# A decoder trunk whose attention layer keeps its tokens by residue class, with the attention values made as seven block products

## The chip, the cores and the metric

One core of a Trainium2 chip runs the whole program. The metric is device time in microseconds of one execution. Five engines matter: TensorE (PE) with its weight loads (PEld), VectorE (DVE), ScalarE (ACT), GpSimd (POOL), and SyncE (SP), which here only issues transfers.

## The reference, cut to what matters

512 tokens of width 1024 pass through two layers. Layer 0 mixes tokens by attention, layer 1 by causal pooling; each is followed by a SwiGLU feed-forward of width 2816.

```python
ATTN_PAIRS = ((128, 1), (512, 4), (2048, 16))     # (window, dilation), 3 groups of 8 heads
def dilated_window_attention(q, k, v, window, dil, slopes):
    # query t attends to keys t - j*dil, j = 0..window/dil; ALiBi bias, softmax
    ...
    o = jnp.einsum('bnhqk,bnkhd->bnqhd', p / den, vb)
    lse = (m + jnp.log(den))[..., 0].transpose(0, 1, 3, 2)
    ...
def dilated_attention_mixer(h, w_qkv, w_out):
    qkv = (h @ w_qkv).reshape(B, S, 3, 3, 8, 128)           # group, q/k/v, head
    ...
    wts = jax.nn.softmax(jnp.stack(lses, axis=0), axis=0)   # over the three groups
    o = jnp.sum(wts[..., None] * o, axis=0).reshape(B, S, ATTN_WIDTH)
    return o.astype(h.dtype) @ w_out
def reference(x, ...):
    x = x + dilated_attention_mixer(rmsnorm(x, attn_norm), w_qkv, w_attn_out)
    x = x + swiglu_ffn(rmsnorm(x, ffn_norm[0]), ...)
    x = x + pooling_mixer(rmsnorm(x, pool_norm), ...)
    x = x + swiglu_ffn(rmsnorm(x, ffn_norm[1]), ...)
    return rmsnorm(x, final_norm)
```

A group with dilation 4 splits the 512 tokens into four residue classes of 128, and the group with dilation 16 works inside the same classes with a stricter mask. Both are called the folded groups below; the group with dilation 1 is the first group.

## The kernel before, in words

**Numbers.** Activations lie transposed: 128 channels on the partitions, 512 tokens along the free dimension, eight such tiles for 1024 channels. Each f32 operand is split into a rounded part (hi, made by ACT, L78) and the rest (lo, made by DVE, L79), and a product is three fp32r products: hi by hi, hi by lo, lo by hi (L245 to L248). Scores, the products with the values and the turning of tiles use full f32; each full-f32 product is two instructions in the trace.

**Weights.** A list of units is built before the program starts. A `Plain` unit is one load of up to 1024 columns and one split. A `Pair` unit (L122) serves a Strassen-Winograd form of two products at once, over 2 x 2 blocks of 512 channels by 256 tokens: three loads from SP and one adding load from POOL, then four steps (blocks, sums, more, last) that make the weight tiles b, s, m and l. Rings of five full and two half split tiles, and four full and two half raw tiles, set how far ahead this runs; `pump` (L165) moves the list on between products.

**Block products.** `seven` (L393) makes two products of 512 columns as seven half products of 4 x 3 matmuls of 256 columns, and DVE adds them up. In the attention layer it serves q and k of heads 1 to 7 (head 1 after its plain start); the feed-forwards use it too. A view (`Straight`, `Folded`) tells it to write a folded group's result with the tokens reordered by residue class.

**Attention.** Head by head q and k of three groups are made; after heads 0, 2, 4, 6 `values` (L496) makes the first group's values of two heads, after heads 1, 3, 5, 7 `values12` (L473) makes those of both folded groups for two heads. In both the normed activations are the stationary operand and the weights the moving one: `values` takes 4 blocks of tokens x 8 chunks x 3 matmuls of 256 columns, `values12` 8 chunks x 4 classes x 3 matmuls of 512 columns, and picks a class out of H with a stride of four tokens. Around these, `between` (L737) and the lists handed to the stages place the other steps of a head: `scores0` (L530) and `scores12` (L564) for scores, exponentials and statistics, which go through DRAM to change between token order and class order; `merge` (L591) for the weights of the groups; `turn` (L611) for transposed probabilities; `output` (L629) for the products with the values, where the folded part is added with a reordering view on DVE (L650). The engines' orders are settled when the program is built, from this order and what is ready.

**Start.** Four leading products run as chunks of x arrive (L709 to L724). Ten instructions on an idle tile (five products, L708) come before. Then a whole product (L725), the sums of squares over channels (`rstd`, L303, one product with a column of ones per 128 tokens), three steps of another product, and the row of scales (`spread`).

**Later stages.** The rest is the output projection, feed-forward 0, the pooling layer and feed-forward 1. The adds into x at the end of a feed-forward are L903.

## Time and profile before

| what | us |
|---|---|
| median of three runs | 1284.84 (1280.31 to 1288.69) |
| the profiled execution | 1277.5 |
| its span, first to last instruction | 1275.7 |
| PE busy in the span | 1262.7 |
| DVE busy | 866.3 |
| ACT busy | 529.4 |
| attention's period for two heads, 206 to 317 | 111.0 |

The granted clock of the profiled execution is 0.998. In a row of time order the first number is the start and the second the length of a group of like instructions, in us; `a<-b,c` names what is written and read, for a matmul the moving and then the stationary operand. In a row of groups the two numbers before the last bar are the busy time in us and the mean length of one in ns. Lengths of matmuls overlap, so a matmul's price is the distance to the next start. A row of stages gives the stretch, its length, then busy time and number of instructions for each engine, the granted clock, the share of the transfer engines, and GB/s. A row of waits gives the total, the number and the longest.

### The profile page before, as it was taken

What the parts mean: (1) busy time and instruction counts of PE and PEld (TensorE: products, weight loads), DVE (VectorE), ACT (ScalarE), POOL (GpSimd) and SP (SyncE); (2) the same over time, 40 slices, a digit from 0 to 9 for tenths busy, and PEclk for the clock granted to TensorE, in tenths of its full rate; (3) what the DMA queues carried; (4) which work ended last, traced back from release to release, by engine and by line L of the source; (5) the groups of instructions that cost most, each with busy time, mean ns of one, the idle gap of its engine ahead of it and who ended that gap; (6) DMA issues with size and microseconds to landing.
All of it is one profiled execution on the core that took longest, in us unless ns stands there. A gap on an engine that the chain in (4) does not pass through costs nothing.

```text
span 1275.7 us, 20125 instructions
## 1 busy us (share of the span) xinstructions
PE 1262.7 (99%) x8036; PEld 1165.3 (91%) x8036; DVE 866.3 (68%) x1313; ACT 529.4 (41%) x825; POOL 106.4 (8%) x105
## 2 busy tenths in 40 slices
PE   9999999999999999999999999999999999999997
PEld 7989999999999998889989999888788988999986
DVE  6794876658566637578636887458978853788643
ACT  6443444444344424445324454333443532455331
POOL 1101101010110100001001110000300000111000
PEclk9999999999999999999999999999999999999999
DMA  8143546446644713147346774333124645676222
GB/s 292 52 142 75 149 133 137 124 110 159 119 117 134 179 53 124 58 100 183 121 141 156 187 180 126 108 139 116 50 67 111 173 139 132 173 182 170 95 69 66
DMA packets 83454, 163.88 MB, mean 128 GB/s; under 512 B 27440, under 2 KB 29504, under 8 KB 83360
## 3 DMA queue, kind: packets, MB, share of 16 engines
q1 hardware_dynamic: 67792, 132.82, 33.4%
q0 software_dynamic: 14416, 28.72, 13.5%
q8 instruction: 63, 1.03, 0.3%
q10 hardware_dynamic: 1152, 1.05, 0.2%
q14 instruction: 31, 0.25, 0.1%
HBM read 160.40 MB, written 2.16 MB: 127 GB/s over the span
## 4 chain that ended last, share of the span: by engine, by line
PE 80%; issue 10%; DVE 6%; DMA 2%; ACT 1%; POOL 1%; SPq 0%; DVEq 0%; POOLq 0%; ACTq 0%
PE ps L385 12%; PE ps L384 12%; PE ps L386 12%; PE ps L245 9%; PE ps L248 9%; PE ps L246 9%; PE ps L484 2%; PE ps L485 2%; PE ps L486 2%; DVE wlo L79 2%; PE ps L647 1%; PE ps L510 1%; PE ps L509 1%; PE ps L511 1%; PE ps L573 1%
## 5 line engine op out<-in xcount | busy, mean ns | idle before, releaser
L79 DVE TENSOR_TENSOR wlo<-raw,whi 128x1024 fp32r<-128x1024 f32 (+2 forms) x286 | 327.0, 1146 | 199.9 <-ACT whi L78 198.8
L78 ACT ACTIVATE whi<-raw 128x1024 fp32r<-128x1024 f32 (+2 forms) x286 | 283.9, 998 | 420.8 <-PE ps L246 203.0
L245 PE MATMUL ps<-a,whi 128*128 128x512 f32 (+1 forms) x374 | 141.0, 377 | 0.0
L246 PE MATMUL ps<-a,whi 128*128 128x512 f32 (+1 forms) x374 | 140.9, 377 | 0.0
L248 PE MATMUL ps<-a,wlo 128*128 128x512 f32 (+1 forms) x374 | 140.8, 377 | 0.0
L384 PE MATMUL ps<-tt,whi 128*128 128x256 f32 x384 | 108.7, 283 | 0.0
L385 PE MATMUL ps<-tt,whi 128*128 128x256 f32 x384 | 108.7, 283 | 0.0
L386 PE MATMUL ps<-tt,wlo 128*128 128x256 f32 x384 | 108.7, 283 | 0.0
L248 PEld LDWEIGHTS ps<-a,wlo 128*128 128x128 f32 x374 | 70.4, 188 | 12.9
L246 PEld LDWEIGHTS ps<-a,whi 128*128 128x128 f32 x374 | 70.4, 188 | 12.8
L245 PEld LDWEIGHTS ps<-a,whi 128*128 128x128 f32 x374 | 70.4, 188 | 12.7
L137 POOL DMA_DIRECT2D raw<-w_pair x32 | 38.3, 1197 | 445.7 <-DVE wlo L79 168.2
L384 PEld LDWEIGHTS ps<-tt,whi 128*128 128x128 f32 x384 | 73.7, 192 | 0.0
L385 PEld LDWEIGHTS ps<-tt,whi 128*128 128x128 f32 x384 | 73.7, 192 | 0.0
L386 PEld LDWEIGHTS ps<-tt,wlo 128*128 128x128 f32 x384 | 73.7, 192 | 0.0
L385 PE MATMUL ps<-tb,whi 128*128 128x256 f32 x256 | 72.6, 284 | 0.5 <-DVE tb L79 0.5
L386 PE MATMUL ps<-tb,wlo 128*128 128x256 f32 x256 | 72.4, 283 | 0.0
L384 PE MATMUL ps<-tb,whi 128*128 128x256 f32 x256 | 72.4, 283 | 0.0
L245 PE MATMUL ps<-h,whi 128*128 128x512 f32 x160 | 62.7, 392 | 0.0
L248 PE MATMUL ps<-h,wlo 128*128 128x512 f32 x160 | 62.3, 389 | 0.0
L246 PE MATMUL ps<-h,whi 128*128 128x512 f32 x160 | 62.3, 389 | 0.0
L384 PE MATMUL ps<-h,whi 128*128 128x256 f32 x216 | 61.9, 286 | 0.0
(247 smaller groups left out, 3329.7 us busy)
## 6 DMA issues: line engine op xcount, KB each, us to landing
raw<-w_pair SPq DMA_DIRECT2D x76, 512.0 KB, 4.2
raw<-w_qkp SPq DMA_DIRECT2D x36, 512.0 KB, 4.7
raw<-w_pair POOLq DMA_DIRECT2D x32, 512.0 KB, 7.1
raw<-w_v SPq DMA_DIRECT2D x24, 512.0 KB, 3.5
raw<-w_down SPq DMA_DIRECT2D x32, 384.0 KB, 3.1
raw<-w_down SPq DMA_DIRECT2D x32, 320.0 KB, 2.8
raw<-w_qkp POOLq DMA_DIRECT2D x18, 512.0 KB, 7.3
rawhalf<-w_pair SPq DMA_DIRECT2D x32, 256.0 KB, 3.3
```

The source lines that it names most:

```text
L78: nc.scalar.activation(hi, v, AF.Copy)
L79: nc.vector.tensor_tensor(lo, v, hi.bitcast(F32), op=OP.subtract)
L137: nc.gpsimd.dma_start(self.b.t.rearrange("p (a c) -> p a c", a=2), self.src[:, None, 3 * S:].to_broadcast([P, 2, S]), accum_op=OP.add)
L245: nc.tensor.matmul(self.p[:, cols], w[0][:, s], mh[:, cols], start=self.done == 0, stop=False)
L246: nc.tensor.matmul(self.p[:, cols], w[0][:, s], ml[:, cols], start=False, stop=False)
L248: nc.tensor.matmul(self.p[:, cols], w[1][:, s], mh[:, cols], start=False, stop=self.done == self.n)
L384: nc.tensor.matmul(dst, w.t[0][:, c], th, start=k == 0, stop=False)
L385: nc.tensor.matmul(dst, w.t[0][:, c], tl, start=False, stop=False)
L386: nc.tensor.matmul(dst, w.t[1][:, c], th, start=False, stop=k == K2 - 1)
L484: nc.tensor.matmul(ps4[b], oph[:, b, :], wh, start=k == 0, stop=False)
L485: nc.tensor.matmul(ps4[b], oph[:, b, :], wl, start=False, stop=False)
L486: nc.tensor.matmul(ps4[b], opl[:, b, :], wh, start=False, stop=k == KC - 1)
```

## The change

**Token order.** In layer 0 tokens lie by residue class: position r * 128 + i * 4 + b holds token b * 128 + i * 4 + r. So x, H, the tiles of sums and everything made from them have each class adjacent, and `block` picks one of the first group's blocks of 128 tokens with a stride of four. The host reorders x and the distance tables to match. The reordering views of `seven`, of head 0's evacuations and of `output` go; `block` comes into head 0's `values`, the first group's scores (both operands), the sums of squares, the row of scales and one ACT copy of `output`. The small transfers of statistics change their patterns. At the end of feed-forward 0 `unfold` adds into x with tokens back in their natural order, into tiles shifted by one, and ACT copies one of them.

**Values.** `values12` becomes the seven block products over two pairs of weights, with activations stationary: 7 x 2 x 4 x 3 matmuls of 256 columns, ACT making one copy and DVE seven sums and differences. The first group's values of heads 2, 4 and 6 become one `seven` with the weights stationary, so they come out transposed, and `turn_values` turns them by eight transposes after the next head's first block product. Head 0's stay plain.

**Order.** Scores of the folded groups and merges are attached to other points of the stages. The start loads the identity and distances from SP after the first weights instead of from POOL before them, runs six idle products instead of five, and makes the sixth product (`begin(1, 0, range(KC))`) after head 0's first evacuations instead of before the sums of squares.

On PE at the start, in the program's names (`early` are the scaled activations, `acc` the sums of squares, `ident` the identity), before:

```order
L245 MATMUL ps_300<-early_94,whi_309 128x512
L246 MATMUL ps_300<-early_95,whi_309 128x512
L248 MATMUL ps_300<-early_94,wlo_310 128x512
L309 MATMUL ps_349<-ones_79,acc_298 128x1 x4
L245 MATMUL ps_358<-early_88,whi_339 128x512 [waits Activation_49]
...
L322 MATMUL ps_383<-ident_78,rcol_356 128x128 [waits DMASW2_49,PE_49,Pool_49]
```

and now:

```order
L257 MATMUL ps_102<-early_95,whi_252 128x512
L259 MATMUL ps_102<-early_94,wlo_253 128x512
L323 MATMUL ps_301<-ones_79,acc_296 128x1 [waits DVE_49]
L323 MATMUL ps_301<-ones_79,acc_296 128x1 x3
L256 MATMUL ps_310<-early_88,whi_319 128x512 [waits Activation_49]
...
L336 MATMUL ps_347<-ident_78,rcol_308 128x128 [waits DMAHW1_49,Pool_49]
```

The sums of squares follow directly on the four leading products, and the row of scales now waits for a transfer from SP's queue.

On DVE in the folded values of heads 2 and 3, where the statistics of a head are merged (`mx`, `ex`), weights are split (`wlo`) and scores prepared (`s`), before:

```order
L575 SCALAR_TENSOR_TENSOR s_2177<-ps,b_2004 128x512 [waits PE_49]
L580 TENSOR_REDUCE st<-s_2177 128x4 [waits DVE_49]
L581 TENSOR_SCALAR nm<-st 128x4 [waits DVE_49]
L79 TENSOR_TENSOR wlo<-raw,whi 128x1024 [waits Activation_49]
L598 TENSOR_TENSOR mx<-st 128x8 [waits DMAHW7_49,DMAHW3_49]
L599 TENSOR_TENSOR ex<-st,mx 128x16 [waits DVE_49]
```

and now (`v` are the values, `sums` and `first` scratch):

```order
L617 TENSOR_SCALAR nm<-st 128x4 [waits DVE_49]
L493 TENSOR_TENSOR v_2268<-ps,first 128x2x256 [waits PE_49,Activation_49]
L80 TENSOR_TENSOR wlo<-raw,whi 128x1024 [waits Activation_49]
L80 TENSOR_TENSOR wlo<-raw,whi 128x1024 [waits DMAHW6_49,Activation_49]
L152 TENSOR_TENSOR raw<-raw 128x512 [waits DMAHW3_49,DMASW3_49,DVE_49]
L153 TENSOR_TENSOR raw<-raw 128x512 [waits DVE_49]
L80 TENSOR_TENSOR wlo<-raw,whi 128x1024 [waits Activation_49] x2
L634 TENSOR_TENSOR mx<-st 128x8 [waits DMAHW7_49,DMAHW4_49]
L635 TENSOR_TENSOR ex<-st,mx 128x16 [waits DVE_49]
L503 TENSOR_TENSOR sums<-ps,first 128x512 [waits PE_49]
```

The merge stands behind three more splits, two sums and an evacuation, and the stage's own evacuations stand behind it.

The diff, cut to its core:

```diff
-WARM = 5
+WARM = 6
...
-            steps.extend([(self, "w", self.blocks), (self, "w", self.sums), (self, "w", self.more),
-                          (self, "half", self.last)])
+        def steps(self):
+            return [(self, "w", self.blocks), (self, "w", self.sums), (self, "w", self.more), (self, "half", self.last)]
...
+    def pairs(*srcs):
+        these = [Pair(src) for src in srcs]
+        for parts in zip(*(p.steps() for p in these)):
+            steps.extend(parts)
+        units.append(these)
...
-        if h % 2 == 0:
-            plain(*[w_v0[h // 2, i] for i in range(2)])
+        if h == 0:
+            plain(w_v0[0], w_v0[1])
+        elif h % 2 == 0:
+            pairs(w_v0p[h // 2 - 1])
         else:
-            plain(*[w_v12[h // 2, i] for i in range(4)])
+            pairs(w_v12[h // 2, 0], w_v12[h // 2, 1])
...
-                nc.tensor.matmul(pc[:, t:t + 1], a[:, t * P:(t + 1) * P], ones,
+                nc.tensor.matmul(pc[:, t:t + 1], block(a, t), ones,
...
-    fold = "p (i r) -> p r i"
-    unfold = "p (r i) -> p r i"
+    def block(t, b, n=1):
+        v = t.rearrange("p (i b) -> p b i", b=NT)
+        return v[:, b] if n == 1 else v[:, b:b + n]
...
+                def product(name, half, key):
+                    p = ps()
+                    for a in range(2):
+                        for k in range(K2):
+                            wh, wl = (v[:, half * S + k % 2 * H2:half * S + (k % 2 + 1) * H2]
+                                      for v in part(unit[k // 2], name).t)
+                            mh, ml = (blk(v, a) for v in T[key, k])
+                            o = both(p)[:, a]
+                            nc.tensor.matmul(o, mh, wh, start=k == 0, stop=False)
+                            nc.tensor.matmul(o, mh, wl, start=False, stop=False)
+                            nc.tensor.matmul(o, ml, wh, start=False, stop=k == K2 - 1)
+                        pump()
+                    return p
...
+                m1 = product("b", 0, "11")
+                first = scratch("first")
+                nc.scalar.copy(first, m1)
+                behind(0)
+                m2 = product("b", 1, "21")
+                nc.vector.tensor_add(quarter(0, 0), both(m2), both(first))
+                done("b")
+                behind(1)
+                m5 = product("s", 0, "1")
...
+                m7 = product("s", 1, "3")
...
+                m6 = product("m", 0, "2")
+                u2 = scratch("sums")
+                nc.vector.tensor_add(u2, m6, first)
+                u3 = scratch("sums")
+                nc.vector.tensor_add(u3, m7, u2)
+                nc.vector.tensor_sub(quarter(1, 1), both(m5), both(u3))
...
-                        mh, ml = (blk(v, b) for v in of(k))
+                        mh, ml = (block(v, b) for v in of(k))
...
+            def turn_values(h):
+                t = apool.tile([P, NT, 2 * P], F32, name="v0")
+                for c in range(2):
+                    p = ps()
+                    for b in range(NT):
+                        nc.tensor.transpose(blk(p, b), block(VT[c], b), ident)
+                    nc.scalar.copy(t[:, :, c * P:(c + 1) * P], p.rearrange("p (b d) -> p b d", b=NT))
+                QKV[h // 2, 0, 2] = t
...
-                    nc.tensor.matmul(blk(p, 2 * b - 2, 2), blk(q0, b), blk(k0, b - 1, 2), start=True, stop=True)
+                    nc.tensor.matmul(blk(p, 2 * b - 2, 2), block(q0, b), block(k0, b - 1, 2), start=True, stop=True)
...
-                nc.tensor.matmul(blk(p, 0, 2), blk(q0, 3), blk(k0, 2, 2), start=True, stop=True)
-                nc.tensor.matmul(blk(p, 2), blk(q0, 0), blk(k0, 0), start=True, stop=True)
+                nc.tensor.matmul(blk(p, 0, 2), block(q0, 3), block(k0, 2, 2), start=True, stop=True)
+                nc.tensor.matmul(blk(p, 2), block(q0, 0), block(k0, 0), start=True, stop=True)
...
-                    nc.sync.dma_start(dn.rearrange("s (b p) -> p s b", p=P), st[:, 0, 0])
-                    nc.sync.dma_start(st[:, 1, 1], dn.rearrange("s (i r) -> i s r", r=4))
+                    nc.sync.dma_start(dn.rearrange("s (p b) -> p s b", b=NT), st[:, 0, 0])
+                    nc.sync.dma_start(st[:, 1, 1], dn.rearrange("s (r p) -> p s r", r=NT))
...
-                nc.scalar.copy(o0, po)
+                nc.scalar.copy(block(o0, 0, NT), po.rearrange("p (b i) -> p b i", b=NT))
...
-                nc.vector.tensor_add(o0.rearrange(fold, r=4), o0.rearrange(fold, r=4), po.rearrange(unfold, r=4))
+                nc.vector.tensor_add(o0, o0, po)
...
-            lead += begin(1, 0, range(KC))
-            rcol = rstd([acc[0]])
+            nc.sync.dma_start(ident, ident_in)
+            nc.sync.dma_start(d0, dist0)
+            nc.sync.dma_start(d12, dist12)
+            rcol = rstd([acc[0]], block)
...
-                    return {0: [later(merge, h - 1)], 1: [later(turn, h - 1), later(scores0, h)], 2: []}[g]
+                    return {0: [later(merge, h - 1), later(turn_values, h - 1)],
+                            1: [later(turn, h - 1), later(scores0, h)], 2: []}[g]
...
                 if h % 2 == 0:
-                    QKV[h // 2, 0, 2] = values(lambda k: H[k], None, {0: [later(scores12, h)]})
+                    VT[:] = [apool.tile([P, S], F32, tag=tag, name="vt") for tag in ("row", "o0")]
+                    seven(T, *VT, scratch, {0: [later(scores12, h)]})
                 elif h < HEADS - 1:
-                    QKV[h // 2, 12, 2] = values12({1: [later(scores12, h)], 5 if h > 1 else 7: [later(merge, h)]})
+                    QKV[h // 2, 12, 2] = values12({0: [later(scores12, h)], 6: [later(merge, h)]})
...
+        def unfold(m, p):
...
+            nc.vector.tensor_add(new.rearrange("p (b i r) -> p r i b", r=NT, b=NT), *(
+                t.rearrange("p (r i b) -> p r i b", r=NT, b=NT) for t in (X[m], p)))
+            X[m] = new
...
-                    nc.vector.tensor_add(X[m], X[m], f.p)
+                    if hf and layer == 0:
+                        unfold(m, f.p)
+                    else:
+                        nc.vector.tensor_add(X[m], X[m], f.p)
```

160 lines of the change are left out of this document (80 added, 80 removed).

## The prediction, made before the changed kernel was timed

> **What bounds the kernel now.** I read the head of the page first, then the stage table, then TensorE (PE) in order of time.
>
> ```profile
> span 1275.7 us, 20125 instructions
> PE 1262.7 (99%) x8036; PEld 1165.3 (91%) x8036; DVE 866.3 (68%) x1313; ACT 529.4 (41%) x825; POOL 106.4 (8%) x105
> PE 80%; issue 10%; DVE 6%; DMA 2%; ACT 1%; POOL 1%; SPq 0%; DVEq 0%; POOLq 0%; ACTq 0%
> ```
>
> PE is busy throughout, and the chain that ended last runs through it. A busy PE may still be slow, so the price of a part is its start-to-start time, and every sum below is made of such differences. The profiled execution took 1277.5 us with this span of 1275.7; the three runs shown have a median of 1284.84, 7.3 us above it. I add the sum to both.
>
> The stage that is replaced four times, the values of the two folded groups, begins at 94.16 and is interrupted by one head's folded scores:
>
> ```profile
> 94.16 0.60 PE L484 MATMUL ps<-whi,h 128*128 128x512 f32 x1
> 94.59 0.40 PE L485 MATMUL ps<-wlo,h 128*128 128x512 f32 x1
> ...
> 100.00 1.95 PE L573 MATMUL ps<-qk,qk 128*128 128x128 f32 x16
> 101.71 0.60 PE L484 MATMUL ps<-whi,h 128*128 128x512 f32 x1
> 102.14 0.40 PE L485 MATMUL ps<-wlo,h 128*128 128x512 f32 x1
> ...
> 118.71 0.39 PE L486 MATMUL ps<-whi,h 128*128 128x512 f32 x1
> 118.94 0.28 PE L384 MATMUL ps<-h,whi 128*128 128x256 f32 x1
> ...
> 129.01 0.27 PE L638 MATMUL ps<-t,v 128*128 128x128 f32 x1
> ```
>
> Its 96 products of 512 columns take 5.84 + 17.23 = 23.07 us. From the second to the last after the scores are 70 steps in 16.57 us: 0.237 us each. The block product that follows (L384 to L386) is 84 products of 256 columns from 118.94 to 129.01: 0.120 each.
>
> **The read that decides.** The old folded stage loads its stationary operand with a stride of four f32; most others load adjacent ones. The profile's two weight-load rows, then the first loads after full-f32 score products:
>
> ```profile
> L484 PEld LDWEIGHTS ps<-whi,h 128*128 128x128 f32 x128 | 40.2, 314 | 0.0
> L509 PEld LDWEIGHTS ps<-whi,early 128*128 128x128 f32 x32 | 6.1, 192 | 0.0
> ```
>
> ```profile
> 50.06 0.19 PEld L509 LDWEIGHTS ps<-whi,early 128*128 128x128 f32 x1
> 50.17 0.19 PEld L510 LDWEIGHTS ps<-wlo,early 128*128 128x128 f32 x1
> ...
> 94.13 0.31 PEld L484 LDWEIGHTS ps<-whi,h 128*128 128x128 f32 x1
> 94.34 0.33 PEld L485 LDWEIGHTS ps<-wlo,h 128*128 128x128 f32 x1
> ```
>
> A strided load lasts 314 ns against 192, and the next load follows after 0.21 us against 0.11. I read 0.237 us as the pace of strided loads: they just hide behind a 512-column product, and would not behind one of 256. That matters because the change removes strided loads from the folded values and puts them into four other places, all behind short products.
>
> The Trainium skill, "SBUF — State Buffer", section "Door 1: The DMA port swizzle", says that SBUF lines are 16 bytes and that each access to a new line pays, with two hits a line needed for full rate; it also lists four f32 as a free stride. The 314 against 192 ns agrees with the first half and not with the list. By the list strided loads would be free, which is the second rival below; by the mechanism the strided moving operand of the scores pays as well.
>
> **The change, part by part.**
>
> *Folded values, four stages.* 96 products of 512 become 7 x 2 x 4 x 3 = 168 of 256 columns, with adjacent weights: 168 x 0.120 = 20.2 us instead of 23.07. Gain 2.85 a stage, **-11.3** for four. The one-sided doubt is whether the weights arrive in time, costed below.
>
> *First-group values, three stages of heads 2, 4, 6.*
>
> ```profile
> 159.05 0.28 PE L509 MATMUL ps<-whi,h 128*128 128x256 f32 x1
> ...
> 161.93 1.95 PE L573 MATMUL ps<-qk,qk 128*128 128x128 f32 x16
> 163.63 0.36 PE L509 MATMUL ps<-whi,h 128*128 128x256 f32 x1
> ...
> 172.34 0.28 PE L384 MATMUL ps<-h,whi 128*128 128x256 f32 x1
> ```
>
> 2.88 + 8.71 = 11.59 us become one block product, 10.07, and eight transposes whose stationary operand is strided. Fifteen transposes with adjacent operands, waits included, took from 90.76 to 92.72, 0.13 each:
>
> ```profile
> 90.76 1.04 PE L618 MATMUL ps<-ident,s 128*128 128x128 f32 x7 [0.21 <-DVE s L606]
> 92.72 1.03 PE L543 MATMUL ps<-qk,qk 128*128 128x256 f32 x4
> 93.58 0.59 PE L548 MATMUL ps<-qk,qk 128*128 128x256 f32 x2
> 94.02 0.38 PE L549 MATMUL ps<-qk,qk 128*128 128x128 f32 x2
> ```
>
> So 8 x 0.13 = 1.0 at best, 8 x 0.237 = 1.9 at the strided pace: -0.5 to +0.4 a stage. I take the strided end, **+1.2** for three (bounds -1.4 and +1.2).
>
> *Head 0's values* stay plain, but now pick every fourth token, so their 96 loads are strided behind 256-column products.
>
> ```profile
> 42.91 0.28 PE L509 MATMUL ps<-whi,early 128*128 128x256 f32 x1
> ...
> 48.66 1.02 PE L543 MATMUL ps<-qk,qk 128*128 128x256 f32 x4
> ...
> 55.92 1.95 PE L573 MATMUL ps<-qk,qk 128*128 128x128 f32 x16
> ```
>
> Between these rows, and without the 1.43 us of scores from 48.66 on, 96 products take 11.58 us. At 0.237 they take 22.7: **+11.1** (bounds 0 and +11.1).
>
> *First-group scores, all eight heads.* The eight instructions from 92.72 to 94.16 (L543, L548, L549) take 1.44 us; a full-f32 product of 256 columns takes two at 0.215. Now q is a strided stationary and k a strided moving operand. If only loads slow down, 8 x 0.237 = 1.9, +0.45 a head, +3.6 in all. If the moving side also halves its rate, as the loads did, six take 0.43 and two stay at 0.237: 3.05 us, +1.6 a head, **+12.9**. No row shows a strided moving operand. The nearest is the strided load: f32 words from the same tiles, 0.84 ns a word adjacent here (0.215 over 256), 0.86 there (0.11 over 128), so I take the halved rate. The bounds are 0 and, should each instruction read every word twice, 6 x 0.86 + 2 x 0.43 - 1.44 = +4.6 a head, +37.
>
> *Row sums of squares* (L309) load the strided accumulator eight times:
>
> ```profile
> 35.58 0.95 PE L309 MATMUL ps<-ones,acc 128*128 128x1 f32 x8
> 36.39 0.49 PE L245 MATMUL ps<-early,whi 128*128 128x512 f32 x1
> ```
>
> 0.81 us become 1.9: **+1.1** (0 to +1.1). The product moved from before to behind this step costs nothing by itself: three steps of another product still cover the root on POOL, and the sums of squares are finished while PE works on the four leading products.
>
> *Start.* Three transfers leave POOL's queue and follow the first weights on SP, ahead of the weights of the next product; a sixth warming matmul is added.
>
> ```profile
> 4.81 1.06 PE L708 MATMUL ps<-idle 128*128 128x256 f32 x2
> 6.41 0.79 PE L245 MATMUL ps<-early,whi 128*128 128x512 f32 x1 [0.54 <-ACT whi L718]
> 7.00 0.63 PE L246 MATMUL ps<-early,whi 128*128 128x512 f32 x1
> 7.43 0.63 PE L245 MATMUL ps<-early,whi 128*128 128x512 f32 x1
> ...
> 10.38 0.39 PE L245 MATMUL ps<-early,whi 128*128 128x512 f32 x1
> ```
>
> From 7.00 on a 512-column product takes 0.43 us, at 118.71 above 0.23; the durations change by 10.38. The moved transfers land while PE has its first 96 products to do, so they delay nobody. The sixth matmul is two more instructions of 0.43 and fills the 0.54 us hole before 6.41. I take **-0.8**, halfway between the whole slow stretch gained (3.6 us at half pace, -1.8) and a start 0.2 later. The Trainium skill, "TensorE: Matmul & The Clock Gate", section "What's actually happening", says the clock opens after some 3.4 us of sustained work, in free-running windows. By that rule the filled hole could open it a window earlier, -1.7 as an estimate, or not, depending on the phase.
>
> *DVE, ACT and queues.* A stage of two pairs splits six tiles of 1024 columns and two of 512 where four of 1024 were split, makes four sums and seven evacuations of 512 columns, and loses four ACT copies.
>
> ```profile
> 206.00:317.00 111.00, 111.00 (x833) 110.61 (x833) 71.85 (x117) 45.13 (x84) 11.83 (x12) 1.00 0.51 127
> 700.00:760.00 60.00, 60.00 (x502) 60.00 (x501) 51.87 (x72) 31.49 (x42) 7.18 (x6) 1.00 0.73 184
> ...
> L79 DVE TENSOR_TENSOR wlo<-raw,whi 128x1024 fp32r<-128x1024 f32 x222 | 270.3, 1220 | 131.4 <-ACT whi L78 131.0
> L150 DVE TENSOR_TENSOR raw<-raw 128x512 f32<-128x512 f32 x50 | 34.2, 684 | 16.7 <-issue 16.4
> DVE mx L598 <- DMA st<-df: 26.9, 7, 10.4
> ```
>
> Two heads take 111 us with DVE busy for 71.85. Added: 2 x 1.22 + 13 x 0.68 = 11.3 for the folded stage, and 1.22 + 6 x 0.68 + 0.4 = 5.7 for the first-group pair. That is 89 of some 112 us, 79%; with 26.9 / 7 = 3.8 us a head spent waiting for the merged statistics, 86%. The feed-forward stage at 700 runs at 86% of DVE without PE losing time, and it loads one pair per 10.1 us, as the new stages do. So this is covered on average, with nothing to spare. The small transfers of statistics swap which hop is scattered and which has runs of four words, which I cost at nothing: only the waiting DVE row could show it. In a stage of two pairs, though, the second pair's tile m is split as the fifth product nears, and a late split stops PE. Late splits are **+1.0** (0 to +6). Layer 0's last feed-forward adds now write strided on DVE and one tile is copied on ACT; each add has 33 products of 0.23 us as its cover, 7.5 us, so nothing, and a fraction of a us where the cover ends.
>
> **Sum:** -11.3 + 1.2 + 11.1 + 12.9 + 1.1 - 0.8 + 1.0 = **+15.2 us**: 1292.7 for a profiled execution, 1300 for a median.
>
> **Rivals.**
>
> *The moving operand pays nothing.* It is fed at half the rate of the split products, which may leave room for line changes. Against it: the loads had the same rate and halved. The scores then cost +3.6 and the sum is +5.9: 1291, within 1%.
>
> *Strided loads are hidden anyway (not slower).* Place: head 0's values, the turns, the scores. For it: 0.237 against about 0.23 is a small loss, and 314 ns could be latency. Against it: the spacing of loads doubled where a product did not hold them up. Then -11.3 - 1.4 - 0.8 + 1.0 = -12.5: 1272. It decides if L509's successor starts its products 0.12 apart.
>
> *DVE becomes the bound in attention.* Its in-order queue stands behind the statistics' DMA while splits wait. At 2 us for each of seven new stages it is +14 instead of +1: 1313. For it: 86% with these waits, which come in one piece. Against it: 86% at 700 without loss.
>
> *Each score instruction reads its words twice.* +37 instead of +12.9: 1324. Nothing in the trace asks for it.
>
> **How the numbers follow.** Chances: forecast 0.47, moving operand free 0.25, loads hidden 0.10, DVE 0.10, read twice 0.08. A measurement here can tell about 1% (12.8 us) from no change. The forecast, at +15.2 with some 4 us either way, is past that in 7 of 10 of its cases; DVE and double reads are too, and hidden loads lie at the edge of faster. That makes slower 0.52, same 0.42, faster 0.06. The range runs from 1285, below the free moving operand, to 1316, above the DVE case; it leaves out hidden loads and double reads.
>
> **What would show it.** Right: the folded values' products 0.12 apart in 20.2 us; head 0's about 0.237 apart with load rows near 314 ns; first-group scores near 3 us a head; DVE near 80% from 100 to 430. Scores near 1.9 us mean the first rival, 0.12 in head 0's values the second; gaps in front of the block products that end on DVE's low parts mean the third. A time below 1285 would refute the forecast.

## The result, and the profile after

The change makes the kernel slower: 1334.71 us (median of six runs, 1330.06 to 1338.09) beside 1283.69 for the kernel before on the same chip (six runs, 1280.31 to 1288.69), a ratio of 1.039 (95% interval 1.036 to 1.042). The forecast was 1300 with a range to 1316. The profiled execution has a span of 1332.4 us against 1275.7, 56.7 more, at a mean granted clock of 0.987 against 0.998. The head of the page after:

```profile
span 1332.4 us, 20898 instructions
PE 1290.3 (97%) x8314; PEld 1182.3 (89%) x8314; DVE 918.6 (69%) x1397; ACT 541.7 (41%) x833; POOL 120.7 (9%) x113
PE 47%; issue 9%; DVE 5%; DMA 3%; ACT 1%; POOL 1%; DVEq 0%; POOLq 0%
```

PE stands idle for 42 us of the span (13 before), and the chain that ended last, 80% PE before, is now 47% PE. I add up, for each function of the kernel, the distance from each matmul's start to the next one's, so that a function's time holds both its work and PE's waits in it:

| part | before, us | after, us | difference | forecast |
|---|---|---|---|---|
| folded values | 92.0 | 81.1 | -10.9 | -11.3 |
| first-group values of heads 2, 4, 6, with turns | 34.8 | 32.9 | -1.9 | +1.2 |
| head 0's values | 11.6 | 22.4 | +10.8 | +11.1 |
| first-group scores | 11.5 | 27.6 | +16.1 | +12.9 |
| sums of squares | 7.1 | 7.9 | +0.8 | +1.1 |
| start and leading products | 73.2 | 70.8 | -2.4 | -0.8 |
| block products in attention, steps over the usual 0.12 us | 0.8 | 23.5 | +22.7 | +1.0, as "late splits", for these four rows together |
| output projection | 44.5 | 55.2 | +10.7 | |
| turned probabilities | 13.1 | 20.7 | +7.6 | |
| folded scores and output | 40.3 | 43.9 | +3.6 | |

(In the row of the first-group values, three block products of 84 x 0.120 = 10.08 us stand for the stages of after.) The rows of work nearly agree with the forecast. The last four, 44.6 us, and some 3 of the 16.1 in the scores come from PE's waits, but not all of it is idle time: that grew by 29 us. In six stretches of the kernel after, from 147.8, 257.0, 342.4, 393.6, 465.2 and 506.2 on and 27.3 us in all, the granted clock is 0.50, each in a wait of PE or just behind waits; the kernel before has none in attention. By the products in them, 0.21 us apart instead of 0.12 (and 0.43 instead of 0.23 for the longer ones), I estimate 10 us more for that. The rest, some 8 us, I have not assigned.

The work first. First-group scores of one head after, in order of time:

```profile
103.31 2.09 PE L579 MATMUL ps<-qk,qk 128*128 128x256 f32 x4
105.22 1.09 PE L584 MATMUL ps<-qk,qk 128*128 128x256 f32 x2
106.14 0.64 PE L585 MATMUL ps<-qk,qk 128*128 128x128 f32 x2
106.42 0.49 PE L471 MATMUL ps<-whi,h 128*128 128x256 f32 x1
```

From 103.31 to 106.42 are 3.11 us; the forecast had 3.05, and 1.44 were before. An instruction of 256 columns takes 1.91 / 4 to 0.92 / 2, 0.46 to 0.48 us, where it took 0.215: the moving operand pays, since strided loads alone pace head 0's products at 0.233 (22.4 / 96). Behind the row stands the rule of the Trainium skill, "SBUF — State Buffer", section "Door 1: The DMA port swizzle": each access to a new 16-byte line pays. The same section's list, in which a stride of four f32 is free, does not agree with these 0.46 us. The weight loads by their form:

```profile
L533 PEld LDWEIGHTS ps<-whi,early 128*128 128x128 f32 x32 | 10.5, 328 | 0.0
L471 PEld LDWEIGHTS ps<-whi,h 128*128 128x128 f32 x96 | 18.4, 192 | 0.0
L554 PEld LDWEIGHTS ps<-ident,vt 128*128 128x128 f32 x24 | 3.1, 210 | 0.0
```

The third number of a row is the mean of one in ns. Head 0's strided loads (L533) last 328, near the 314 of the strided loads of before; those of the folded values, now adjacent, last the 192 of the adjacent loads of before.

Now the waits. The transfers of statistics, before and then after, with the median from issue to landing as the last number:

```profile
dn<-st SPq DMA_DIRECT2D x8, 4.0 KB, 10.3
st<-dn SPq DMA_DIRECT2D x8, 4.0 KB, 3.5
df<-st SPq DMA_DIRECT2D x8, 4.0 KB, 4.3
st<-df SPq DMA_DIRECT2D x8, 4.0 KB, 2.8
```

```profile
dn<-st SPq DMA_DIRECT2D x8, 4.0 KB, 3.2
st<-dn SPq DMA_DIRECT2D x8, 4.0 KB, 5.7
df<-st SPq DMA_DIRECT2D x8, 4.0 KB, 11.6
st<-df SPq DMA_DIRECT2D x8, 4.0 KB, 3.5
```

Each moves the same 4 KB. A write in single words takes 10 to 12 us, one in runs of four words 3 to 4. Before, the write in single words was that of the first group (`dn`), issued 19 to 27 us ahead of the merge. After, it is that of the folded groups (`df`), the last thing that the merge waits for; before, it was issued only 6 to 9 us ahead of it. "DMA: Bandwidth & Descriptors" of the Trainium skill, section "Rules for kernel authors", says that a non-contiguous last dimension becomes one descriptor per element; the writes agree, 11.6 against 3.2 us, and so do the packets under 512 B: 27792 in the kernel after, 21648 in the run below that makes the `df` write in runs, which is 6144 or 8 x (1024 - 256) fewer. The waits of the kernel after, on DVE and ACT and then on SP (us in all, times, longest):

```profile
DVE mx L634 <- DMA st<-df: 64.8, 8, 12.0
ACT ex L636 <- DVE ex L635: 66.0, 8, 12.6
```

```profile
SPq L624 <- DMA df<-st: 88.1, 8, 13.1
```

SP stands 11 us a head before it may issue the read, DVE 8.1 us in each of eight heads before the merge (3.8 in each of seven before), and ACT behind DVE. The last head's merge shows what that does to PE. In order of time, on SP, on DVE and on PE, with a row of the granted clock (third number from its end) behind the wait:

```profile
486.90 0.38 SPq L623 DMA_DIRECT2D df<-st  x1
487.33 0.57 SPq L115 DMA_DIRECT2D raw<-w_out  x1
497.45 0.38 SPq L624 DMA_DIRECT2D st<-df  x1
```

```profile
493.82 0.69 DVE L505 TENSOR_TENSOR sums<-ps,sums 128x512 f32<-128x512 f32 x1
506.55 0.17 DVE L634 TENSOR_TENSOR mx<-st 128x8 f32<-128x8 f32 x1 [12.04 <-DMA st<-df]
506.63 0.68 DVE L506 TENSOR_TENSOR v<-ps,sums 128x512 f32<-128x512 f32 x1
507.24 0.68 DVE L511 TENSOR_TENSOR first<-ps,sums 128x512 f32<-128x512 f32 x1
507.83 1.21 DVE L80 TENSOR_TENSOR wlo<-raw,whi 128x1024 fp32r<-128x1024 f32 x1
508.96 0.68 DVE L512 TENSOR_TENSOR v<-first,ps 128x512 f32<-128x512 f32 x1
509.56 0.68 DVE L80 TENSOR_TENSOR oh<-o,oh 128x512 fp32r<-128x512 f32 x1
```

```profile
502.26 0.50 PE L256 MATMUL ps<-oh,whi 128*128 128x512 f32 x1 [1.53 <-ACT oh L79]
510.30 0.79 PE L257 MATMUL ps<-oh,whi 128*128 128x512 f32 x1 [7.54 <-DVE oh L80]
510.89 0.63 PE L259 MATMUL ps<-oh,wlo 128*128 128x512 f32 x1
511.32 0.63 PE L256 MATMUL ps<-oh,whi 128*128 128x512 f32 x1
```

```profile
511.00:514.00 3.00, 3.00 (x12) 2.61 (x11) 2.90 (x10) 0.22 (x1) 0.00 (x0) 0.50 0.70 227
```

The write is issued at 486.90. DVE is at the merge from 494.5 on, waiting for 12.04 us; three evacuations, a weight split and the low part of a head's output (`oh`) stand behind it. PE lacks that `oh` from 502.8 on, waits 7.54 us, and then makes products at 0.43 us each, half pace, at a clock of 0.50. This wait is the longest of the eight and not all the write's: the read behind it took 9.1 us here (497.45 to 506.55), against a median of 3.5.

### The profile page after: what moved, and what is told of

Same layout as the page of the kernel before. It is cut to its first block, busy times and chain, and to the rows that moved or that the text cites. A ratio compares the mean times of both kernels' runs of the same rounds, so it can differ in the third digit from the quotient of the medians.

```text
span 1332.4 us, 20898 instructions
## 1 busy us (share of the span) xinstructions
PE 1290.3 (97%) x8314; PEld 1182.3 (89%) x8314; DVE 918.6 (69%) x1397; ACT 541.7 (41%) x833; POOL 120.7 (9%) x113
## 2 busy tenths in 40 slices
DMA packets 88321, 172.57 MB, mean 130 GB/s; under 512 B 27792, under 2 KB 30240, under 8 KB 88224
## 3 DMA queue, kind: packets, MB, share of 16 engines
q0 software_dynamic: 17264, 34.09, 16.1%
## 4 chain that ended last, share of the span: by engine, by line
PE 47%; issue 9%; DVE 5%; DMA 3%; ACT 1%; POOL 1%; DVEq 0%; POOLq 0%
PE ps L257 8%; PE ps L259 8%; PE ps L256 8%; PE ps L369 7%; PE ps L370 7%; PE ps L371 7%; DMA raw<-w_pair 1%; DVE wlo L80 1%; DMA df<-st 1%; DMA st<-df 1%; DVE n L304 1%; POOL rcol L328 0%; DVE raw L423 0%; PE ps L336 0%; DVE x L1020 0%
## 5 line engine op out<-in xcount | busy, mean ns | idle before, releaser
L79 ACT ACTIVATE whi<-raw 128x1024 fp32r<-128x1024 f32 (+2 forms) x297 | 293.9, 999 | 456.3 <-PE ps L257 182.8
L80 DVE TENSOR_TENSOR wlo<-raw,whi 128x1024 fp32r<-128x1024 f32 (+2 forms) x297 | 339.8, 1149 | 165.4 <-ACT whi L79 164.1
L369 PE MATMUL ps<-h,whi 128*128 128x256 f32 x252 | 75.7, 300 | 9.5 <-ACT t L655 6.2
L259 PEld LDWEIGHTS ps<-a,wlo 128*128 128x128 f32 x374 | 70.4, 188 | 12.9
L371 PE MATMUL ps<-h,wlo 128*128 128x256 f32 x252 | 73.3, 291 | 0.0
L370 PE MATMUL ps<-h,whi 128*128 128x256 f32 x252 | 73.1, 290 | 0.0
L256 PE MATMUL ps<-h,whi 128*128 128x512 f32 x160 | 62.7, 392 | 0.0
## 6 DMA issues: line engine op xcount, KB each, us to landing
raw<-w_down SPq DMA_DIRECT2D x32, 384.0 KB, 3.4
```

What stands on the lines that cost most here:

```text
L79: nc.scalar.activation(hi, v, AF.Copy)
L80: nc.vector.tensor_tensor(lo, v, hi.bitcast(F32), op=OP.subtract)
L256: nc.tensor.matmul(self.p[:, cols], w[0][:, s], mh[:, cols], start=self.done == 0, stop=False)
L259: nc.tensor.matmul(self.p[:, cols], w[1][:, s], mh[:, cols], start=False, stop=self.done == self.n)
L369: nc.tensor.matmul(dst, w.t[0][:, c], th, start=k == 0, stop=False)
L370: nc.tensor.matmul(dst, w.t[0][:, c], tl, start=False, stop=False)
```

## The experiments

Theory A: the slow write lies just ahead of the merge, the merge holds DVE's and ACT's order, and what stands behind it comes late for PE. Theory B: DVE has too much work in attention with two pairs of weights at once. A third, raised later: it is SP's queue that the transfer holds, with weight loads behind it. Times are medians, beside those of the kernel before in the same session, with the ratio and its 95% interval. The kernel before differs by up to 7.4 us between sessions, so runs of different sessions are compared by their distance to it.

| run | us | before | ratio |
|---|---|---|---|
| the change | 1334.71 | 1283.69 | 1.039 [1.036, 1.042] |
| df_runs | 1288.02 | 1279.90 | 1.007 [1.005, 1.009] |
| before_scatter | 1310.91 | 1279.90 | 1.025 [1.021, 1.030] |
| scores_blocks | 1333.68 | 1279.90 | 1.041 [1.038, 1.044] |
| h0_adjacent | 1313.36 | 1279.90 | 1.027 [1.024, 1.029] |
| df_reads | 1291.90 | 1278.24 | 1.010 [1.007, 1.013] |
| df_scores | 1286.86 | 1278.24 | 1.006 [1.004, 1.008] |
| df_scores_h0 | 1282.25 | 1278.24 | 1.004 [1.002, 1.005] |
| merge_late | 1318.25 | 1278.24 | 1.030 [1.027, 1.034] |
| merge_pinned | 1296.04 | 1278.84 | 1.014 [1.011, 1.017] |
| read_pool | 1342.99 | 1278.84 | 1.050 [1.047, 1.053] |
| all_pinned | 1273.80 | 1278.84 | 0.997 [0.995, 0.998] |
| scores_after_two | 1273.88 | 1277.58 | 0.997 [0.996, 0.998] |
| df_scores_rows | 1282.87 | 1276.27 | 1.005 [1.003, 1.007] |
| all_rows | 1268.52 | 1276.27 | 0.993 [0.992, 0.995] |
| all_rows_two | 1268.50 | 1278.23 | 0.991 [0.989, 0.994] |

### The write alone, undone and done

df_runs, an edit of the kernel after:

```diff
-nc.sync.dma_start(df.rearrange("s (r p) -> p s r", r=NT), st[:, 0, 1])
+nc.sync.dma_start(df.rearrange("s (p r) -> p s r", r=NT), st[:, 0, 1])
```

> The changed kernel, in which only the write of the folded groups' statistics to DRAM (df<-st) has its old form, four adjacent words for each partition and quantity, in place of single words; the read back is as changed, so the statistics land at other tokens and the weights of the groups are not the reference's. In the trace of the changed kernel this write is the slow one of the four transfers (11.6 us from issue to landing, 4.3 before), and the merge of the statistics waits 64.8 us for the read behind it where it waited 26.9. Theory A, slow write ahead of the merge: it holds DVE's in-order queue, and the splits and evacuations behind the merge are late for PE. Then df<-st falls to about 3 us, the merge's wait from 64.8 to under 20 us, and most of the 48 us of waits on PE go: 1290 to 1305 us. Theory B, DVE has too much work in attention with two pairs of weights (DVE busy 918.6 against 866.3 us): the wait falls, the splits stay late, 1325 us or more.

The transfer and the merge's wait in its trace:

```profile
df<-st SPq DMA_DIRECT2D x8, 4.0 KB, 4.6
```

```profile
DVE mx L634 <- DMA st<-df: 8.9, 5, 3.9
```

The distance to the kernel before falls from 51.0 us to 8.1: one transfer's access pattern is worth 43 us. The work of DVE is the same as in the change (919.0 against 918.6 us busy), so theory B alone does not make these 43 us. The profiled execution has no stretch at half clock in attention either. The 8.1 us that are left are nearly the sum of the work terms: here the steps of the block products over the usual pace are back at 2.0 us, and the scores, undisturbed, stand at 24.9, +13.4 (forecast +12.9). With that, the six rows of work are -10.9 - 1.9 + 10.8 + 13.4 + 0.8 - 2.4 = +9.8.

before_scatter, the reverse edit in the kernel before:

```diff
-nc.sync.dma_start(df.rearrange("s (i r) -> i s r", r=4), st[:, 0, 1])
+nc.sync.dma_start(df.rearrange("s (r i) -> i s r", r=4), st[:, 0, 1])
```

> The kernel before, in which only the write of the folded groups' statistics to DRAM (df<-st) is made in single words, as the change makes it; the read back is as before, so the statistics land at other tokens and the weights of the groups are not the reference's. The write should take about 11 us where it took 4.3. Theory A in its plain form, the slow write alone is enough: the merge's wait grows from 26.9 by about 7 us a head to 80 us, and the time by 25 to 50 us, to 1310 or more. Theory B, and also A if the wait only hurts where DVE is filled to the brim by the pairs: DVE has 72 of 111 us to do, the wait is absorbed, within 8 us of before.

```profile
df<-st SPq DMA_DIRECT2D x8, 4.0 KB, 10.9
```

```profile
DVE mx L598 <- DMA st<-df: 80.9, 8, 14.1
```

The slow write is enough by itself: +31 us on a kernel that has nothing else of the change. The merge waits even longer than in the change (80.9 against 64.8 us) and the time suffers less (31 against 43). That a DVE with fewer splits to do catches up better, so much of theory B, would explain it, but is not shown: the merges also stand at other places in this kernel.

### What exactly is held

merge_late and merge_pinned both keep the slow write. merge_late moves the calls, one block product later:

```diff
-return {0: [later(merge, h - 1), later(turn_values, h - 1)],
-        1: [later(turn, h - 1), later(scores0, h)], 2: []}[g]
+return {0: [later(turn_values, h - 1)], 1: [later(merge, h - 1)],
+        2: [later(turn, h - 1), later(scores0, h)]}[g]
...
-values12({0: [later(scores12, h)], 6: [later(merge, h)]})
+values12({0: [later(scores12, h)]})
```

> The changed kernel with the slow write, but each merge of statistics (but the last head's) is placed one block product, 10 us, later in the program, with the turn and the output behind it. Theory A, DVE and ACT are held in their order by a merge that came too early for its data: the merge's wait falls from 64.8 us to about 15, the stalls in attention go, and what stays is the last head's merge, some 11 us in the output projection: 1295 to 1308 us. Rival, it is SP's queue that the transfer holds (SP waits 88.1 us for df<-st before it issues the read, with weight loads behind): the stalls stay, 1325 or more.

Head 5 in its trace, on SP and on DVE:

```profile
354.44 0.36 SPq L623 DMA_DIRECT2D df<-st  x1
365.94 0.36 SPq L624 DMA_DIRECT2D st<-df  x1
```

```profile
355.04 2.36 DVE L80 TENSOR_TENSOR wlo<-raw,whi 128x1024 fp32r<-128x1024 f32 x2 [0.15 <-ACT whi L79]
367.86 0.17 DVE L634 TENSOR_TENSOR mx<-st 128x8 f32<-128x8 f32 x1 [10.46 <-DMA st<-df]
368.16 0.69 DVE L503 TENSOR_TENSOR sums<-ps,first 128x512 f32<-128x512 f32 x1
```

The expectation was wrong: 40 us over before, and the merge waits 61.4 us in all. DVE is at the merge at 357.4, 3 us after the write was issued, and the evacuations of the folded values (L503), whose call comes before the merge's, stand behind it. So the call's place is not what puts the merge there. The order of DVE's queue is made when the program is built, and by these rows it seems to count on a quick transfer. Hence the next edit, a data dependence instead of a place (`behind` gives the last column of the last evacuation ahead of the merge in the program):

```diff
+nc.vector.tensor_copy(mx[:, 0, :1], behind())
 nc.vector.tensor_max(mx, st[:, 0, :, 0, :], st[:, 1, :, 0, :])
...
```

> The changed kernel with the slow write, and one tiny DVE copy ahead of each merge that reads the last evacuation made before the merge in the program, so that the merge cannot stand earlier than that on DVE. In the changed kernel, and also where the merge was written one product later (1318 us), DVE came to the merge only 3 to 7 us after the write of the statistics was issued, though the program has 17 us between them; so the order on DVE was not the program's, and moving the call moved it little. Write, read and landing take 11.6 + 3.5 and a little: with the copy DVE comes some 17 us after the write and should find them there. Theory A, the engine's order held by a merge put ahead of its data: its wait falls from 64.8 to under 20 us and the time to 1290 to 1305 us, with the write still at 11 us. Rival, the transfer holds SP's queue and the weights behind it: 1318 or more.

```profile
df<-st SPq DMA_DIRECT2D x8, 4.0 KB, 10.4
```

```profile
SPq L625 <- DMA df<-st: 82.8, 8, 14.2
```

The write is as slow as ever and SP waits for it nearly as long, but no wait of DVE for it is left in the list, and the distance to before is 17.2 us: 34 of the 43 come back without touching the transfer. That speaks against SP's queue as well. The run made for that question issues the read from POOL:

```diff
-nc.sync.dma_start(st[:, 1, 0], df.rearrange("s (p b) -> p s b", b=NT))
+nc.gpsimd.dma_start(st[:, 1, 0], df.rearrange("s (p b) -> p s b", b=NT))
```

> The changed kernel with the slow write, and the read of the folded groups' statistics issued from POOL's queue, so that SP does not stand 11 us before it. Theory A (DVE and ACT behind the merge): the merge waits as long, 1325 us or more. Rival (SP's queue, with weight loads behind the read): 1290 to 1310.

```profile
POOL st L624 <- DMA df<-st: 124.1, 8, 41.8
DVE mx L634 <- DMA st<-df: 69.8, 8, 13.3
```

SP is free, the merge waits as long, and the time rises to 64 us over before: POOL's queue, which adds the fourth load of each pair, is now the one that stands, so this run alone would not clear SP's queue. With merge_pinned the rival falls: there SP waits 82.8 us and most of the time comes back. A wait inside an in-order queue costs what PE needs from behind it.

### The work terms

scores_blocks writes q and k of the first group in the order of its blocks (`apart`, a reordering view in `seven` and in head 0's evacuations), h0_adjacent takes adjacent tokens in head 0's values:

```diff
-block(q0, b), block(k0, b - 1, 2)
+blk(q0, b), blk(k0, b - 1, 2)
...
-nc.vector.tensor_add(both(one), both(p26), twice(first[:, :H2]))
+nc.vector.tensor_add(apart(one), both4(p26), twice4(first[:, :H2]))
...
```

```diff
-mh, ml = (block(v, b) for v in of(k))
+mh, ml = (blk(v, b) for v in of(k))
```

> The changed kernel, in which q and k of the first group are written in the order of its blocks by the same DVE operations (with a stride in the view that is written), so that the scores of that group read adjacent words; nothing else is changed. The strided scores take 0.459 us an instruction of 256 columns against 0.215 and cost 16.1 us in all, 12.3 of it by their pace. If that price is real, the scores return to 1.4 us a head and the time falls by 12 to 16 us, to 1319 to 1323. If the strided writes of DVE cost as much as they save (DVE being behind), the scores get faster and the time stays within 5 us of 1334.7.

> The changed kernel, in which the plain values of head 0 take adjacent tokens as the stationary operand in place of every fourth, so that the values of heads 0 and 1 belong to other tokens than the reference's. Its 96 products should go from 0.233 to 0.120 us each, 22.4 to 11.6 us, and the time fall by 10.8 us to 1324, if the price is that of the strided weight loads. If PE there in truth waits for DVE, which prepares the operands of the next stages at that time, the products stay slow or the time lost turns up behind them: less than 4 us gained.

The scores went from 27.6 to 20.6 us of PE's time, 11.7 without waits, and nothing was gained (53.8 us over before, the change 51.0): the block products' steps over the usual pace went from 23.5 to 32.4, and the stretches at a clock of 0.50 from 27.3 to 47.8 us. I read this as a PE that arrives earlier at the same wait, but the run does not show it alone: the reordering view also gave DVE more to do (926.2 us busy against 918.6). Head 0's products went from 22.4 to 11.7 us as expected, but the distance to before fell by 17.5 us, from 51.0 to 33.5: the waits in the block products shrank too, from 23.5 us to 12.3, with the merge's wait at 56.7 in place of 64.8. The clock accounts for most of the surplus: h0_adjacent has two stretches at 0.50, 13.7 us in all, in place of six with 27.3, which by the estimate above loses 3 us in place of 10. Why its waits are fewer is open, so the 17.5 cannot be counted as the price of head 0's loads.

So these terms can only be measured with the waits gone. df_reads puts the statistics at the right tokens with the write in runs; df_scores adds the block order, df_scores_h0 makes head 0's values with the weights stationary and turns them:

```diff
+nc.sync.dma_start(df.rearrange("s (p r) -> p s r", r=NT), st[:, 0, 1])
+by_class = df.rearrange("s (i b r) -> s r i b", b=NT, r=NT)
+for r in range(NT):
+    for s in range(2):
+        nc.sync.dma_start(st[r * NI:(r + 1) * NI, 1, 0, s], by_class[s, r])
```

```diff
+nc.tensor.matmul(p, wh, mh, start=k == 0, stop=False)
+nc.tensor.matmul(p, wh, ml, start=False, stop=False)
+nc.tensor.matmul(p, wl, mh, start=False, stop=k == KC - 1)
...
+nc.vector.tensor_mul(VT[c], p, rows["row"])
...
```

> The changed kernel, with the folded groups' statistics written to DRAM in runs of four words as in the run that only changed this write (1288.0 us beside 1279.9 for the kernel before), and read back at the right tokens by eight small transfers of 32 x 4 single words, so that the weights of the groups are the reference's. Theory A, the slow write ahead of the merge: reads of single words took 5.7 us where runs took 3.5, and SP issues eight in place of one at some 0.4 us each, so the merge waits 3 to 5 us a head longer than with the permuted read; whether PE feels it depends on what DVE has in hand: 1288 to 1300. Theory B, too much work on DVE, fell with the first run and expects the same here.

> The changed kernel with the statistics written in runs and read by eight transfers, and with q and k of the first group written in block order, so that its scores read adjacent words. With the slow write in place the block order moved the time by nothing (1333.7 against 1334.7 us), though its score instructions went from 27.6 to 20.6 us with waits, 11.7 without: the stalls behind the merge had taken up what the scores gave. If that reading is right, here, with the merge early, the gain shows in full: 12 to 14 us less than the run with the eight reads alone. If DVE's strided writes eat it, less than 5.

> As the run with runs, eight reads and block order, and the plain values of head 0 made with the weights stationary and the activations moving (48 products of 512 columns), scaled by DVE and turned by eight transposes like the values of the later heads. 48 x 0.237 + 8 x 0.12 = 12.3 us in place of 22.4: 10 us less than that run, some 1264 to 1272, and faster than the kernel before by over 1% if the run with runs lies at 1288. If PE then waits for the operands that DVE prepares in that stage, half of it or less.

df_reads lands inside its expectation, 13.7 us over before where df_runs had 8.1. The other two gain 5.0 and 4.6 us where 12 to 14 and 10 were expected (5.0 is nearly the lower case of df_scores), though PE's own time fell in full (scores 24.9 to 12.7, head 0's values 22.4 to 11.0 and 0.85 for its turns). The rest went into new stalls, and DVE's rows of df_scores and then of df_scores_rows show part of the reason:

```profile
L417 DVE TENSOR_TENSOR qk<-ps,first 128x512 f32<-128x512 f32 x12 | 8.2, 684 | 0.0
L415 DVE TENSOR_TENSOR qk<-ps,first 128x512 f32<-128x512 f32 x6 | 6.5, 1088 | 0.0
```

```profile
L418 DVE TENSOR_TENSOR qk<-ps,first 128x512 f32<-128x512 f32 x6 | 4.1, 682 | 0.0
```

My view wrote the block order with a stride, 1088 ns for what takes 684 in the other groups. Writing rows of adjacent words, and reading PSUM with the stride, takes 682:

```diff
-return t.rearrange("p (b a i) -> p a i b", a=2, b=NT)
+return t.rearrange("p (b a i) -> p a b i", a=2, b=NT)
...
-return t.rearrange("p (a i b) -> p a i b", a=2, b=NT)
+return t.rearrange("p (a i b) -> p a b i", a=2, b=NT)
...
```

> The run with runs, eight reads and block order (1286.9 us), in which DVE writes the block order as rows of adjacent words and has its stride in what it reads from PSUM. If the strided writes were the price, the operations return from 1064-1088 to some 685 ns, 1.4 us a head on DVE, the three stalls of 2.2 to 3.4 us behind the turned probabilities shrink, and the time falls to 1278 to 1282. If the weights are late for a faster PE, the operations get shorter and the stalls stay: 1284 to 1288.

1282.87 us, 6.6 over before in place of 8.6; the two intervals overlap, so the gain is 2 us or not certain at all, and the expected 1278 to 1282 is missed. The stalls behind the turned probabilities did shrink, from 7.6 us to 4.7, but they are not gone:

```profile
PE ps L369 <- ACT t L684: 4.7, 3, 1.7
PE ps L635 <- DVE qk L436: 3.7, 3, 1.2
```

### A version faster than both

all_pinned has the write in runs with the eight reads, the block order, head 0's values turned and the pinned merge; all_rows the adjacent rows besides. Two more place the folded groups' scores one block product later:

```diff
-seven(T, *VT, scratch, {0: [later(scores12, h)]})
+seven(T, *VT, scratch, {1: [later(scores12, h)]})
```

```diff
-values12({0: [later(scores12, h)], 6: [later(merge, h, lambda: V12[0][:, 1, S - 1:])]})
+values12({1: [later(scores12, h)], 6: [later(merge, h, lambda: V12[0][:, 1, S - 1:])]})
...
-values12({0: [later(scores12, h)], 1: [later(halve, 0), later(halve, 1)],
+values12({1: [later(scores12, h), later(halve, 0), later(halve, 1)],
...
```

> The run with runs, eight reads, block order and head 0's values turned (1282.3 us, with 14 us of stalls in the block products, three of them 2.4 to 3.1 us, when the copies of turned probabilities on ACT stand behind the split of a weight that has not landed), and the pinned merge besides. If those stalls come from the merges' place, 1268 to 1274, faster than the kernel before by up to 1%. If they come from weights that land too late for a PE that has become faster, which the pin does not touch, 1280 to 1286 as without it.

> The run with everything and the pinned merge (1273.8 us), with the folded groups' scores of heads 2, 4 and 6 placed after the second block product of the next pair in place of the first. There PE waited 1.84 us three times for DVE's evacuation of the q and k that the scores read (5.1 us in all): one block product is 1.44 us more of cover. If that is all, 4 to 5 us less, 1268 to 1270, and 0.7% under the kernel before. If the scores' later end moves the statistics and the merge so that DVE is late elsewhere, no change, 1272 to 1276.

> The run with everything and the pinned merge (1273.8 us), with the same rows of adjacent words. There PE waits 5.1 us in three places for DVE's evacuation of the folded groups' q and k and 2 us for copies on ACT. With 1.4 us a head less on DVE, if DVE sets those waits: 1268 to 1271. If they are set by the place that the scores have on PE, right behind the first block product: 1272 to 1275.

> The run with everything and rows of adjacent words (1268.5 us), with the folded groups' scores of heads 3, 5 and 7 placed after the second block product of the folded values in place of the first: there, and not in heads 2, 4 and 6, the trace shows PE waiting for DVE's evacuation of q and k, 1.3 and 1.8 us. If a block product of folded values (2.88 us) as cover is what is missing, both waits go: 3 us less, 1264.5 to 1266.5. If DVE is behind by its work, the wait moves to another product: 1267 to 1270.

all_pinned came to 1273.8, at the upper end of what was expected if the stalls come from the merges' place. scores_after_two was aimed badly and gained nothing (3.7 us under before): its trace shows the waiting scores in heads 3, 5 and 7, 24 matmuls into the folded values, and the edit had moved those of 2, 4 and 6. all_rows came to 1268.5, the lower of its two cases, 7.8 us under before where all_pinned was 5.0. all_rows_two moved the right scores; their waits went (17.0 us of folded scores to 13.6), and the time stayed at 1268.5 (the two ratios' intervals overlap), with 2.2 us more in the block products and 2.1 in the turned probabilities:

```profile
span 1267.9 us, 20930 instructions
PE 1251.9 (99%) x8274; PEld 1152.8 (91%) x8274; DVE 919.7 (73%) x1407; ACT 545.4 (43%) x831; POOL 121.1 (10%) x113
```

By the end a few us of waiting move with the scores instead of going; that DVE's amount of work sets them, theory B, fits this but is not shown by a run of its own. The best versions are 0.7 to 0.9% faster than the kernel before, for a change whose first form was 3.9% slower.

## Why the prediction was wrong

**What held.** The reading that strided operands decide the work: folded values -10.9 (forecast -11.3), head 0 +10.8 (+11.1), scores +13.4 undisturbed (+12.9), sums of squares +0.8 (+1.1). The rivals "moving operand pays nothing", "strided loads are hidden anyway" and "reads its words twice" are refuted by the 0.46 us of a score instruction, where they would have 0.237 or 0.86, and by head 0's products 0.233 us apart in place of 0.120. Two small terms were too high: the first-group values gained 1.9 us where a loss of 1.2 was taken, because the turning transposes are hardly slowed by their stride (24 in 2.7 us), and the start gained 2.4, not 0.8. Of that gain some 1.6 us may be chance: eight leading products stand 0.4 us apart in the trace of before, and 0.23 in that of before_scatter, which has the same start. Work alone, as in df_runs, would have ended at 1.007 of before, 1293 on the forecast's base of 1284.84, within the range.

**The step that failed** is the one sentence that the transfers of statistics "swap which hop is scattered and which has runs of four words, which I cost at nothing", and with it "Late splits are **+1.0** (0 to +6)". The swap costs 43 us. The splits as such were sized well: with the write in runs the block products' steps are 2.0 us over the usual pace, 1.2 more than before; what the term had nothing for is the merge that holds them. Its price stood in the rows of before that I did not read: a scattered write 10.3 us, one in runs 4.3. The write before the merge takes that much longer for each of eight heads, 7.3 us by the medians (11.6 - 4.3); and the DVE row that I did quote, 26.9 us of waiting in the merge, already said that DVE comes to the merge ahead of its data, with no slack to lose. 26.9 + 8 x 7.3 would have been 85 us of waiting for DVE, close to the 80.9 of before_scatter; a merge that has its data late holds both engines that feed PE.

**The third rival** had the right place, word for word, an in-order queue that "stands behind the statistics' DMA while splits wait", with a chance of 0.10 and a price of 2 us for each of seven stages, +14. The waits cost 47 us with what followed from them, 10.7 of it in the output projection, and the chance was put low by an argument from shares: DVE at 86% in a feed-forward stage loses nothing. From 700 to 760 the longest wait on DVE is 1.1 us, where the merge's are 7.4 to 12 in seven heads of eight. A share of busy time says nothing about a wait in one piece.

**Its bounds were one-sided.** I gave the strided operands bounds from nothing to a double read, and the transfers none, because the two swapped. Two hops that swap their prices are even only if the same amount of slack lies behind each.

## What to carry to other kernels

When a change alters the access pattern of a small transfer, price each hop from its row of DMA issues (issue to landing) and ask which of them lies ahead of the next consumer; moving the scattered hop from the early transfer to the late one cost 43 us here for 4 KB a head. A tiny instruction that waits for a round trip through DRAM holds everything behind it in its engine's order, and writing its call later did not move it there: a data dependence did, and brought 34 us back with the transfer as slow as before. Take waits away before measuring what work costs, since work taken from PE while it waits for another engine returned nothing in one run here and more than its price in another.

## What the runs showed of the hardware that was not expected

A moving f32 operand with a stride of four words takes 0.46 us for 256 columns against 0.215, and a stationary one 316 to 328 ns a load against 192; yet the eight transposes of a pair, whose stationary operand has the same stride, load in 210 ns and follow each other after 0.11 to 0.12 us, as adjacent ones do. On DVE a stride costs where it writes SBUF (1088 ns against 684) and not where it reads PSUM (682). It costs in what DVE reads from SBUF too: in df_scores the sums that write adjacent words and read `qk` with the stride (L422) take 1064 ns against 686 in the other groups.

PE's pace drops after waits shorter than I had thought harmless. In the kernel after, a wait, and then the granted clock in a stretch ahead of it and one behind it (the third number from a row's end):

```profile
254.26 0.28 PE L371 MATMUL ps<-tx,wlo 128*128 128x256 f32 x1
256.31 0.39 PE L369 MATMUL ps<-t,whi 128*128 128x256 f32 x1 [1.77 <-DVE sums L503]
```

```profile
253.00:254.20 1.20, 1.20 (x12) 1.20 (x12) 0.00 (x0) 0.00 (x0) 0.00 (x0) 1.00 1.00 235
257.40:260.40 3.00, 3.00 (x16) 3.00 (x16) 2.93 (x10) 1.81 (x4) 1.17 (x1) 0.50 0.32 49
```

A hole of 2.05 us between two starts was followed, 0.7 us later, by 3.4 us at a clock of 0.50, with products 0.21 us apart where 0.12 is the pace. Two holes of 1.4 us close together (ending at 391.1 and 392.8) were followed by such a stretch as well; single ones of 1.53 and 1.80 us (at 231.1 and 384.0), and one of 2.54 us in merge_late (at 376.0), by none. The Trainium skill, "TensorE: Matmul & The Clock Gate", section "HAM oscillation — how this bites in real kernels", gives as its rule that gaps should stay under some 3.4 us; here 2 us were enough in some places, and the runs do not show what tells them apart.
